# A two-layer decoder kernel: output products with high priority, expert results stored by block, residuals first in the last stage's memory

## The chip, the cores and the metric

The kernel runs on one core of a Trainium2 chip. The metric is the device time of one execution in microseconds; the lower the better. In the profile PE is the matrix engine, DVE the vector engine, ACT the scalar engine, POOL the GpSimd engine and SP the engine that issues most of the DMAs.

## The reference

Two layers on 2048 tokens of width 1024, batch 1. Each layer mixes tokens and then applies a mixture of experts, and both steps end in a layer norm of the scaled residual plus the result:

```python
x = layer_norm(alpha * x + mixer(x))       # layer 0: sliding-window attention, layer 1: latent attention
x = layer_norm(alpha * x + hier_moe(x))    # 32 experts in 4 groups, 2 per token, hidden width 512

xs = xt[tok_sorted]                        # tokens sorted by expert
hid = silu(ragged_dot(xs, w_gate, sizes)) * ragged_dot(xs, w_up, sizes)
ys = ragged_dot(hid, w_down, sizes) * weight[order]
out = segment_sum(ys, tok_sorted)          # back to the tokens, two rows each
```

All inputs and outputs are float32.

## The kernel before

**Numbers.** Matrix products take each float32 operand as a high and a low float16 half and make three products of them (`mm3`, L196 to L198; for the experts L898 to L900 and L914 to L916). ACT cuts off the high half (`wh`, L171) and DVE or POOL the low half (`wl`, L176 or L174).

**Stages.** Tokens come in 16 tiles of 128. For layer 0, `swa` (0 to some 470 us of the span) computes the attention and writes its transposed result `aoT` to the DRAM array `o`; `project` multiplies by the output weights, adds the residual, normalizes, routes, and scatters each token's row into the slots of its experts (array `xs`); `moe` (from some 706 us) runs 32 experts. For layer 1, `mla` first adds up the experts' results of layer 0, then attends (to some 2575 us), and `project` and `moe` (2820 to 3513 us) follow again. `combine_last` (from 3513 us) adds the two expert rows of each token to the residual, normalizes and writes the output.

**Slots.** Every expert has `SLOT` = 192 rows in `xs` and in its result array `y` (`y0` for layer 0, `y1` for layer 1). `CAPS` is the number of rows that the kernel computes for an expert: 184 for one, 176 for four, 160 for six, 152 for five, 144 for seven and 128 for nine, the larger ones for the experts with more tokens. Rows behind `CAPS` that hold tokens are treated by a loop (`overflow`) that runs only if there are any. In `swa` a DMA per expert (L401, two for each tile) clears the upper half of its `xs` rows.

**An expert.** Six weight pieces of 1 MB each (tile `raw`, five buffers, loaded by SP at L828) are cut into halves; `up` and `down` multiply; DVE transposes the result into `yr` (L918), and `store` writes it with four POOL DMAs (L926) of 192 KB, always all 6 blocks of 32 rows. `yr` is one of three fixed tiles, whose blocks behind the 128th row were cleared once per layer by POOL (L941).

**Output products.** In `project` (L263) the loads of tile t+2, the products of tile t and its norm are written in one loop (`skew`). `load` takes the attention's result `o` (two buffers) and the residual `pxr`; `gemm` makes two halves of 24 matmuls each and adds each half to `pxr` at L294. Only layer 0's first two loads of `o` are under `tc.high_priority()`.

**The last stage.** `combine_last` loads all 16 residual tiles `cz0` to `cz15` (L1090) ahead, gathers two rows for each token (`cy0`, `cy1`, nine buffers each; POOL, L1066), adds them (`cz`, two DVE operations at L1073), and normalizes. `layer_norm_shared` needs ACT twice, DVE at L248, L250 and L251, a reciprocal square root on POOL (`pow`, L252), and then DVE at L253.

**Order.** The order of the instructions on each engine is fixed when the kernel is built: the framework simulates a timeline with its own costs, and the instruction that is ready first in it, or has priority, goes first in the engine's queue. At run time each queue is strictly in order. A pool's place in memory decides which earlier tile's last use a new tile waits for, so pools matter for the order too.

Of the kernel before, what the change touches and what calls it, by code (L numbers as in the profile page):

```python
# [9 lines left out]
F32 = mybir.dt.float32  # L10
# [11 lines left out]
P = 128  # L22
# [98 lines left out]
class Kernel:  # L121
# [141 lines left out]
    def project(self, i, w_o, o_view, res, x_out, xs_d, rp, weights, early):  # L263

        nc, tc = self.nc, self.tc
        with ExitStack() as s:
# [10 lines left out]
            T, sent = {}, []  # L277

            def load(t):
                with tc.high_priority() if i == 0 and t < 2 else ExitStack():  # L280
                    ov = o_view(op, t)
                xr = self.t(wk, [P, D], F32, "pxr", bufs=3)
                nc.sync.dma_start(xr, res[t * P:(t + 1) * P, :])
                T[t] = {"o": ov, "xr": xr}

            def gemm(t):
                o, xr = T[t]["o"], T[t]["xr"]
                for n in range(2):
                    cs = slice(n * 512, (n + 1) * 512)
                    py = self.t(pm, [P, 512], F32, "mm")  # L290
                    for c in range(KC):
                        self.mm3(py, o[:, 0, c], o[:, 1, c], wh[c][:, cs], wl[c][:, cs], c == 0, c == KC - 1)

                    nc.vector.scalar_tensor_tensor(xr[:, cs], xr[:, cs], ALPHA * WS, py, op0=ALU.mult, op1=ALU.add)  # L294
# [63 lines left out]

        return (wh, wl), load

    def swa(self, xt_d, o_d, w_o, xs_d, keep):

        nc, tc, a = self.nc, self.tc, self.a
        V, G, C = nc.vector, nc.gpsimd, nc.scalar
# [1 line left out]
        with ExitStack() as s:  # L366
# [25 lines left out]

            zero = self.t(wk, [P, D], F16, "zero", bufs=1)
            G.memset(zero, 0.0)
            rooms, cleared = xs_d.rearrange("(e s) (u c) -> e s u c", s=SLOT, u=2)[:, SLOT // 2:], []

            def clear(t):
                one = T[t]["xl"][0:1, 0, 0:1]
                V.tensor_tensor(zero[0:1, 0:1], one, one, op=ALU.is_lt)
                for e in range(t, NE, NT):  # L400
                    cl = nc.sync.dma_start(rooms[e], zero[:SLOT // 2, None, :].to_broadcast([SLOT // 2, 2, D]))  # L401
                    for q in cleared:
                        tc.declare_no_dep(cl.ins, q.ins, reason="other rows")
                    cleared.append(cl)

            pick = self.after[:, None, :].bitcast(I32).to_broadcast([P, 2, P])
            upto = self.upto[:, None, :].to_broadcast([P, 8, P])
# [454 lines left out]
    def moe(self, i, x_d, xs_d, y_d, held, rp, weights, first):  # L862
# [3 lines left out]
        ids, blocks = rp["ids"], lambda e: -(-CAPS[e] // 32)  # L866
        xs = xs_d.rearrange("(e s) c -> e s c", s=SLOT)
        ys = y_d.rearrange("(e b i) (a k) -> e a i b k", b=CB, i=32, a=4)
        X, H = {}, {}
        with ExitStack() as s:  # L870
            wp = s.enter_context(tc.tile_pool(name=f"mw{i}", bufs=1, reuse_waits="tile"))
            xk = s.enter_context(tc.tile_pool(name=f"mx{i}", bufs=3, side="right", reuse_waits="tile"))
# [32 lines left out]

            def down(e, q):
                hh, hl = H[e]
                py, yr = pys[q], yrs[e % 3]
                for d in range(2):
                    out = py[:, d, :CAPS[e]]  # L910
                    cs = slice((2 * (q % 2) + d) * P, (2 * (q % 2) + d + 1) * P)
                    for m in range(F // P):
                        hi, lo = (w.rearrange("p (m d) -> p m d", m=F // P)[:, m, cs] for w in W[e, 4 + q // 2])
                        nc.tensor.matmul(out, hi, hh[:, m], start=m == 0, stop=False)  # L914
                        nc.tensor.matmul(out, hi, hl[:, m], start=False, stop=False)  # L915
                        nc.tensor.matmul(out, lo, hh[:, m], start=False, stop=m == F // P - 1)  # L916
                for d in range(2):
                    nc.vector.transpose(yr[:, :blocks(e), (2 * q + d) * 32:(2 * q + d + 1) * 32],  # L918
                                        py[:, d, :32 * blocks(e)].rearrange("p (b i) -> p b i", i=32))
                if q == 3:  # L920
                    store(e)

            def store(e):
                to = self.expert(ids, e, mybir.EngineType.Pool)
                for a in range(4):
                    st = nc.gpsimd.dma_start(ys[to, a].rearrange("o i b k -> (o i) b k"), yrs[e % 3][32 * a:32 * a + 32])  # L926
                    for q in stored:
                        tc.declare_no_dep(st.ins, q.ins, reason="other rows")
                    stored.append(st)
                for x in (H, X):  # L930
                    x.pop(e)

            stored = []
# [2 lines left out]
            pys = [self.t(ps, [P, 2, 256], F32, f"py{n}") for n in range(4)]  # L936
            for p in pys:
                nc.vector.memset(p[:, :, CAPS[0]:CAPB], 0.0)
            yrs = [self.t(wk, [P, CB, 256], F32, f"yr{n}", bufs=1) for n in range(3)]
            for y in yrs:  # L940
                nc.gpsimd.memset(y[:, min(CAPS) // 32:], 0.0)  # L941
            for u in range(4 * NE + BEHIND):
                e, m = divmod(u, 4)
                cut_to(u - 1)
# [135 lines left out]
    def combine_last(self, i, x_d, y_d, out):  # L1080
        nc, tc = self.nc, self.tc
        with ExitStack() as s:
            yp, c, zp, wk = (s.enter_context(tc.tile_pool(name=f"{n}{i}", bufs=bufs, reuse_waits="tile"))
                             for n, bufs in (("cy", 9), ("cl", 1), ("cz", 1), ("cw", 4)))
            T = [{} for _ in range(NT)]
            g, b = self.load_ln(c, i, 1)

            def load_x(t):
                T[t]["z"] = self.t(zp, [P, D], F32, f"cz{t}")
                nc.sync.dma_start(T[t]["z"], x_d[t * P:(t + 1) * P, :])  # L1090

            for t in range(NT):
                load_x(t)

            def load(t):
                self.combine_rows(t, yp, y_d, T[t])

            def norm(t):
                d = T[t]
                self.combine_sum(t, d)  # L1100
                if t > NT - 3:
                    self.layer_norm(wk, d["z"], d["x"], g, b, 1.0 / ALPHA)
                else:
                    self.layer_norm_shared(wk, d["z"], d["x"], g, b, 1.0 / ALPHA)
                nc.sync.dma_start(out[t * P:(t + 1) * P, :], d["x"])

            skew(NT, (load, 0), (norm, 6))
# [432 lines left out]

def scratch(k, pool):
    d = {n: k.t(pool, [rows, D], F32, n) for n, rows in
         (("x1", S), ("x2", S), ("x3", S), ("xc", S), ("y0", ROWS), ("y1", ROWS))}
    d["wd"] = k.t(pool, [2 * S, 1], F32, "wd")
    d["xs"] = k.t(pool, [ROWS, 2 * D], F16, "xs")
    d["o"] = k.t(pool, [NT, P, 2 * D], F16, "o")
    d["ob"] = k.t(pool, [KC, P, 2, S], F16, "ob")
    d["q"] = k.t(pool, [4, 3, P, 2, S], F16, "q")
    d["kr"] = k.t(pool, [ROPE, 2, S], F16, "kr")
    return d  # L1550
# [45 lines left out]
def trunk(tc, a, out):  # L1596
    with ExitStack() as ctx:
# [1 line left out]
        d = scratch(k, ctx.enter_context(tc.tile_pool(name="dram", bufs=1, space=DRAM)))  # L1599
        k.constants(ctx)  # L1600
        keep = ExitStack()
        w_o = k.swa(a["x_t"], d["o"], a["a_w_o"][0], d["xs"], keep)
        feed_forward(k, tc, 0, w_o, tile_of(k, d["o"]), a["x"][0], d["x1"], d["xs"], d["y0"], (d["xc"], d["wd"]), 7, keep)
        keep = ExitStack()
        w_o = k.mla(d["x1"], d["y0"], d["x2"], d, keep)
        feed_forward(k, tc, 1, w_o, chunk_of(k, d["ob"]), d["x2"], d["x3"], d["xs"], d["y1"], (d["xc"], d["wd"]), 5, keep)
        k.combine_last(1, d["x3"], d["y1"], out[0])


def expert_pieces(inputs):  # L1610
# [35 lines left out]
```

## Time and profile before

| | us |
|---|---|
| median of 3 runs | 3634.66 |
| lowest and highest | 3625.09, 3639.14 |
| the profiled execution | 3634.45 |
| its span, in which the rows' times count | 3632.5 |

The granted clock of PE is given as a share of full speed, 0.923 in the mean over the span. The rows below are of five kinds. In the page's slices each digit is a fortieth of the span, in tenths. In a table by stretch each engine has its busy microseconds and its number of instructions, and behind them stand the granted clock, the DMA engines' share and their rate. In lists of waits a row has the waiting engine and line, what ended the wait, the sum, the count and the longest. In a timeline a row has the start, the duration, engine, line, operation, tiles written and read, how many in a row, and in brackets the idle time before it with what ended that. An issue row of SP (SPq) tells when SP handed a DMA over, and not how long the transfer took.

### The profile page before, as it was taken

Reading aid. Unit: us, or ns where it says so; the run is one execution under the profiler, and the core shown is the slowest. Engines: PE = TensorE matmul, PEld = TensorE weight load, DVE = VectorE, ACT = ScalarE, POOL = GpSimd, SP = SyncE. Lnnn points to the kernel's source line nnn. Section 1 sums busy time; section 2 is a strip of 40 time slices with the busy share of each in tenths; the row PEclk is TensorE's granted clock in tenths of the full one; section 3 lists DMA queues with packets and bytes.
Section 4 is the critical chain, followed back from the end, with each engine's and each line's share of the span. In section 5 each row is a group of like instructions: output and inputs, shape, how many; then the busy total and the mean of one; then the engine's idle time right before and its main releaser. Section 6 shows DMA issues by size and latency. Waiting matters only on the chain. (4 is left out here: it accounts for less than half of the span.)

```text
span 3632.5 us, 83064 instructions
## 1 busy us (share of the span) xinstructions
PE 2978.4 (82%) x32611; PEld 2241.4 (62%) x32611; DVE 2765.4 (76%) x5272; ACT 2109.8 (58%) x3669; POOL 1563.2 (43%) x1568
## 2 busy tenths in 40 slices
PE   7888788699988885688898888888886899888850
PEld 3445443399988884344566556565443899888850
DVE  5777767788777786675788888788586788787758
ACT  6666621266666774443777777677210666666743
POOL 3545334322222335564576666566144133322344
PEclk9999899799998997899999999999998899999975
DMA  7877679899999998997899999899698999999995
GB/s 209 173 167 154 134 225 313 257 346 339 343 354 359 358 360 270 223 219 183 140 194 182 171 167 178 160 181 188 175 302 243 281 363 350 361 359 361 355 355 207
DMA packets 1108729, 931.59 MB, mean 256 GB/s; under 512 B 933120, under 2 KB 991744, under 8 KB 1057408
## 3 DMA queue, kind: packets, MB, share of 16 engines
q1 hardware_dynamic: 1073504, 808.65, 83.3%
q0 software_dynamic: 34816, 117.47, 8.9%
q8 instruction: 259, 4.24, 0.5%
q14 instruction: 150, 1.23, 0.1%
HBM read 538.32 MB, written 159.65 MB: 192 GB/s over the span
## 5 line engine op out<-in xcount | busy, mean ns | idle before, releaser
L176 DVE SCALAR_TENSOR_TENSOR wl<-raw,wh 128x2048 f16<-128x2048 f32 x322 | 838.7, 2608 | 196.5 <-ACT wh L171 196.3
L898 PE MATMUL pg<-xt,wh 128*128 128x128 f16 (+5 forms) x4096 | 827.7, 232 | 58.9 <-DMA xt<-xs 28.1
L900 PE MATMUL pg<-xt,wl 128*128 128x128 f16 (+5 forms) x4096 | 814.7, 232 | 46.4 <-DVE wl L176 46.3
L899 PE MATMUL pg<-xt,wh 128*128 128x128 f16 (+5 forms) x4096 | 827.4, 232 | 0.0
L171 ACT ACTIVATE wh<-raw 128x2048 f16<-128x2048 f32 x384 | 723.9, 1901 | 117.1 <-DMA raw<-in_moe_w_dram 112.6
L1416 POOL TENSOR_TENSOR bpp<-bpr,bpp 128x512 f16<-128x512 f32 (+3 forms) x448 | 474.2, 1077 | 273.8 <-DVE bpp L1413 173.3
L916 PE MATMUL py<-hh,wl 128*128 128x128 f16 (+5 forms) x2048 | 415.2, 231 | 48.7 <-POOL wl L174 48.7
L926 POOL DMA_DIRECT2D y<-yr x256 | 145.3, 569 | 716.0 <-DVE yr L918 424.0
L900 PEld LDWEIGHTS <-wl 128*128 128x128 f16 x4096 | 405.6, 100 | 57.9 <-DVE wl L176 57.7
L898 PEld LDWEIGHTS <-wh 128*128 128x128 f16 x4096 | 408.1, 100 | 44.9 <-issue 31.1
L1389 DVE TENSOR_REDUCE bsm<-sc 128x1 f32<-128x512 f32 (+3 forms) x640 | 373.1, 601 | 80.4 <-PE sc L1386 60.3
L899 PEld LDWEIGHTS <-wh 128*128 128x128 f16 x4096 | 408.4, 100 | 17.0 <-issue 17.0
L915 PE MATMUL py<-hl,wh 128*128 128x128 f16 (+5 forms) x2048 | 414.8, 230 | 4.6 <-DVE hl L174 4.5
L914 PE MATMUL py<-hh,wh 128*128 128x128 f16 (+5 forms) x2048 | 413.8, 230 | 1.6 <-ACT wh L171 1.3
L1398 ACT ACTIVATE bpr<-sc,bsm 128x512 f32<-128x512 f32 (+3 forms) x640 | 352.5, 630 | 90.4 <-DVE bsm L1394 84.4
L174 POOL TENSOR_TENSOR wl<-raw,wh 128x2048 f16<-128x2048 f32 x62 | 253.4, 4087 | 266.1 <-ACT wh L171 244.9
L1447 PE MATMUL po<-v,bpt 128*128 128x130 f16 x1750 | 205.3, 223 | 79.5 <-DMA bpt<-bpp 72.8
L1384 PE MATMUL sc<-kb,qb 96*128 96x512 f16 (+3 forms) x640 | 232.8, 364 | 29.8 <-DVE ro L1289 12.4
L916 PEld LDWEIGHTS <-wl 128*128 128x128 f16 x2048 | 202.9, 99 | 60.1 <-POOL wl L174 55.0
L1385 PE MATMUL sc<-kb,qb 96*128 96x512 f16 (+3 forms) x640 | 232.3, 363 | 0.0
L1386 PE MATMUL sc<-kb,qb 96*128 96x512 f16 (+3 forms) x640 | 230.8, 362 | 0.0
L1447 PEld LDWEIGHTS <-bpt 128*128 128x128 f16 x1750 | 160.0, 98 | 112.0 <-DMA bpt<-bpp 94.7
(324 smaller groups left out, 7771.7 us busy)
## 6 DMA issues: line engine op xcount, KB each, us to landing
raw<-in_moe_w_dram SPq DMA_DIRECT2D x384, 1024.0 KB
y<-yr POOLq DMA_DIRECT2D x256, 192.0 KB
x<-pxr SPq DMA_DIRECT2D x32, 512.0 KB
cz<-x SPq DMA_DIRECT2D x32, 512.0 KB
xs<-zero SPq DMA_DIRECT2D x32, 384.0 KB
q<-qn SPq DMA_DIRECT2D x48, 256.0 KB
ax<-in_x_t_dram SPq DMA_DIRECT2D x16, 512.0 KB
o<-aoT SPq DMA_DIRECT2D x16, 512.0 KB
```

The source lines that it names most:

```text
L171: nc.scalar.activation(hi, src, AF.Copy, scale=scale)
L176: eng.scalar_tensor_tensor(lo, src, scale, hi, op0=ALU.mult, op1=ALU.subtract)
L898: nc.tensor.matmul(out, hi, x[:, c], start=c == 0, stop=False)
L899: nc.tensor.matmul(out, hi, x[:, KC + c], start=False, stop=False)
L900: nc.tensor.matmul(out, lo, x[:, c], start=False, stop=c == KC - 1)
L914: nc.tensor.matmul(out, hi, hh[:, m], start=m == 0, stop=False)
L915: nc.tensor.matmul(out, hi, hl[:, m], start=False, stop=False)
L916: nc.tensor.matmul(out, lo, hh[:, m], start=False, stop=m == F // P - 1)
L1389: V.tensor_reduce(sm[:, c:c + 1], sc[:, :w], axis=AX.X, op=ALU.max, negate=ncn == 1)
L1398: C.activation(pr[:, :w], sc[:, :w], AF.Exp, bias=nm)
L1416: (V if mine[1] else G).tensor_tensor(pp[:, :, 1], pb, pp[:, :, 0], op=ALU.subtract)
L1447: nc.tensor.matmul(po, pt[:, k % 4, 0], vv, start=k == 0, stop=False)
```

## The change

In `project` the loads of `o` and of the residual and the products of tiles 0 and 1 get high priority in both layers. The results `y0` and `y1` become one array `y`; `store` writes only the blocks of 32 rows that `CAPS` of the expert covers, so that of 192 blocks per layer 36 (of 128 KB each) are no longer written, and `yr` becomes an ordinary tile of a pool with three buffers without clearing. Instead `swa` clears rows 128 to 191 of each expert in `y` (two DMAs of 256 KB per tile, 32 in all). In `combine_last` the pools are opened in another order, so that the residuals `cz` take the lowest addresses and `cy` the place they had.

```diff
@@ project @@
             def load(t):
-                with tc.high_priority() if i == 0 and t < 2 else ExitStack():
+                with tc.high_priority() if t < 2 else ExitStack():
                     ov = o_view(op, t)
-                xr = self.t(wk, [P, D], F32, "pxr", bufs=3)
-                nc.sync.dma_start(xr, res[t * P:(t + 1) * P, :])
+                    xr = self.t(wk, [P, D], F32, "pxr", bufs=3)
+                    nc.sync.dma_start(xr, res[t * P:(t + 1) * P, :])
                 T[t] = {"o": ov, "xr": xr}

             def gemm(t):
+                with tc.high_priority() if t < 2 else ExitStack():
+                    product(t)
+
+            def product(t):
                 o, xr = T[t]["o"], T[t]["xr"]
@@ swa @@
+            least, swept = min(CAPS) // 32 * 32, []
+            sums = y_d.rearrange("(e s) (u c) -> e s u c", s=SLOT, u=2)[:, least:]
...
+                    cl = nc.sync.dma_start(sums[e], zero.bitcast(F32).rearrange("p (u c) -> p u c", u=1)[:SLOT - least].to_broadcast([SLOT - least, 2, D // 2]))
+                    for q in swept:
+                        tc.declare_no_dep(cl.ins, q.ins, reason="other rows")
+                    swept.append(cl)
@@ moe @@
             def down(e, q):
                 hh, hl = H[e]
-                py, yr = pys[q], yrs[e % 3]
+                if q == 0:
+                    Y[e] = self.t(wk, [P, CB, 256], F32, "yr", bufs=3)
+                py, yr = pys[q], Y[e]
...
-                    st = nc.gpsimd.dma_start(ys[to, a].rearrange("o i b k -> (o i) b k"), yrs[e % 3][32 * a:32 * a + 32])
+                    st = nc.gpsimd.dma_start(ys[to, a, :, :blocks(e)].rearrange("o i b k -> (o i) b k"), Y[e][32 * a:32 * a + 32, :blocks(e)])
...
-            yrs = [self.t(wk, [P, CB, 256], F32, f"yr{n}", bufs=1) for n in range(3)]
-            for y in yrs:
-                nc.gpsimd.memset(y[:, min(CAPS) // 32:], 0.0)
@@ combine_last @@
-            yp, c, zp, wk = (s.enter_context(tc.tile_pool(name=f"{n}{i}", bufs=bufs, reuse_waits="tile"))
-                             for n, bufs in (("cy", 9), ("cl", 1), ("cz", 1), ("cw", 4)))
+            zp, c, yp, wk = (s.enter_context(tc.tile_pool(name=f"{n}{i}", bufs=bufs, reuse_waits="tile"))
+                             for n, bufs in (("cz", 1), ("cl", 1), ("cy", 9), ("cw", 4)))
@@ scratch @@
-         (("x1", S), ("x2", S), ("x3", S), ("xc", S), ("y0", ROWS), ("y1", ROWS))}
+         (("x1", S), ("x2", S), ("x3", S), ("xc", S), ("y", ROWS))}
```

The order that is built moves at these places. First SP's queue where layer 0's attention ends. `apt` and `aoT` are transposes by DMA of the last attention tiles, `o<-aoT` a store of the attention's result, `o_...<-o` the loads for the first products, `lng`, `lnb` and `wr` constants of the norm and the router. Line numbers of the changed kernel are higher: its L1574 is L1565, its L543 is L533. Before:

```order
L180 DMA_TRANSPOSE aoT_1007_5762<-aop_1006_5759 128x16x128
L1565 DMA o_1045_5927<-o_9_65 128x2048
L1565 DMA o_1047_5931<-o_9_65 128x2048
L180 DMA_TRANSPOSE apt_993_5657<-app_992_5654 128x8x128
L180 DMA_TRANSPOSE apt_1001_5710<-app_1000_5707 128x8x128
L533 DMA o_9_65<-aoT_1007_5762 128x2048
L219 DMA lng_1049_5935<-in_ln_g_dram 128x1024
L220 DMA lnb_1050_5936<-in_ln_b_dram 128x1024
L258 DMA wr32_1051_5939<-in_moe_w_group_dram 128x8x4
```

With the change:

```order
L1574 DMA o_1044_5958<-o_8_64 128x2048
L1574 DMA o_1046_5962<-o_8_64 128x2048
L219 DMA lng_1048_5966<-in_ln_g_dram 128x1024
L220 DMA lnb_1049_5967<-in_ln_b_dram 128x1024
L258 DMA wr32_1050_5970<-in_moe_w_group_dram 128x8x4
L180 DMA_TRANSPOSE apt_992_5688<-app_991_5685 128x8x128
L180 DMA_TRANSPOSE aoT_1006_5793<-aop_1005_5790 128x16x128
L180 DMA_TRANSPOSE apt_1000_5741<-app_999_5738 128x8x128
L543 DMA o_8_64<-aoT_1006_5793 128x2048
```

Three constants and one `aoT` now stand ahead of the last transposes of the attention. On PE the first output product stands in both kernels behind the last attention matmul, in both layers.

Second DVE's queue in the last stage, from its first sum to the first L253, which waits for POOL's first `pow`. L1082 of the changed kernel is L1073. Before, all of it:

```order
L1073 SCALAR_TENSOR_TENSOR cz0_6311_53116<-cy0_6327_53148,w12_23_95,cz0_6311_53116 128x1024
L1073 SCALAR_TENSOR_TENSOR cz0_6311_53116<-cy1_6328_53152,w12_23_95,cz0_6311_53116 128x1024
L248 TENSOR_SCALAR lnms_6341_53206<-lnms_6341_53206 128x1
L250 SCALAR_TENSOR_TENSOR cz0_6311_53116<-cz0_6311_53116,lnms_6341_53206,lng_6309_53112 128x1024
L251 TENSOR_SCALAR lnms_6341_53206<-lnms_6341_53206 128x1
L1073 SCALAR_TENSOR_TENSOR cz1_6312_53118<-cy0_6329_53156,w12_23_95,cz1_6312_53118 128x1024
L1073 SCALAR_TENSOR_TENSOR cz1_6312_53118<-cy1_6330_53160,w12_23_95,cz1_6312_53118 128x1024
L248 TENSOR_SCALAR lnms_6345_53226<-lnms_6345_53226 128x1
L253 SCALAR_TENSOR_TENSOR cz0_6311_53116<-cz0_6311_53116,lnms_6341_53206,lnb_6310_53113 128x1024
```

With the change, its last rows up to the first L253:

```order
L1082 SCALAR_TENSOR_TENSOR cz4_6372_53207<-cy1_6393_53267,w12_22_94,cz4_6372_53207 128x1024
L1082 SCALAR_TENSOR_TENSOR cz5_6373_53209<-cy0_6394_53271,w12_22_94,cz5_6373_53209 128x1024
L250 SCALAR_TENSOR_TENSOR cz3_6371_53205<-cz3_6371_53205,lnms_6410_53349,lng_6366_53195 128x1024
L251 TENSOR_SCALAR lnms_6410_53349<-lnms_6410_53349 128x1
L1082 SCALAR_TENSOR_TENSOR cz6_6374_53211<-cy0_6396_53279,w12_22_94,cz6_6374_53211 128x1024
L1082 SCALAR_TENSOR_TENSOR cz5_6373_53209<-cy1_6395_53275,w12_22_94,cz5_6373_53209 128x1024
L253 SCALAR_TENSOR_TENSOR cz0_6368_53199<-cz0_6368_53199,lnms_6398_53289,lnb_6367_53196 128x1024
```

Before, four sums and one L250 stand ahead of the first L253; now thirteen sums (tiles 0 to 5 and one of tile 6) and four L250. On POOL 20 gathers stand ahead of the first `pow` before, and 22 now.

## Rows read from the trace of the kernel before

**Rows 1.** Page, part 2: the span in 40 slices.
```profile
DMA  7877679899999998997899999899698999999995
```

**Rows 2.** Table by stretch (us; busy and count per engine; clock, DMA share, GB/s).
```profile
200.00:300.00 100.00, 86.48 (x596) 48.60 (x593) 75.52 (x181) 69.69 (x242) 46.83 (x73) 0.91 0.85 173
```

**Rows 3.** Timeline of SP in `swa`: clears of three tiles, and a weight load.
```profile
113.79 0.33 SPq L356 DMA_DIRECT2D worw<-in_a_w_o_dram  x1
114.21 1.27 SPq L401 DMA_DIRECT2D xs<-zero  x2
...
304.84 1.27 SPq L401 DMA_DIRECT2D xs<-zero  x2
...
387.09 1.28 SPq L401 DMA_DIRECT2D xs<-zero  x2
```

**Rows 4.** Waits from 50 to 440 us: waits for transposes by DMA.
```profile
DVE apt L504 <- DMA apt<-app: 66.1, 40, 3.6
...
PE sc L484 <- DMA qT<-qs: 27.1, 13, 3.7
```

**Rows 5.** Timelines of SP and of PE where layer 0's attention ends.
```profile
461.28 3.36 SPq L180 DMA_TRANSPOSE apt<-app  x2
...
465.47 0.44 SPq L219 DMA_DIRECT2D lng<-in_ln_g_dram  x1
...
465.81 0.29 PE L516 MATMUL po<-vv,apt 128*128 128x128 f16 x1 [5.76 <-DMA apt<-app]
```

**Rows 6.** Waits of DVE from 466 to 520 us: the first residual of layer 0.
```profile
DVE pxr L294 <- DMA pxr<-in_x_dram: 8.6, 1, 8.6
```

**Rows 7.** Timeline of PE, layer 1's first output products.
```profile
2578.84 0.61 PE L196 MATMUL mm<-ck,o 128*128 128x512 f16 x1 [6.53 <-DMA o<-ob]
...
2584.05 0.38 PE L196 MATMUL mm<-ck,o 128*128 128x512 f16 x1
2584.27 0.38 PE L197 MATMUL mm<-kst,o 128*128 128x512 f16 x1
```

**Rows 8.** Table by stretch, columns as in rows 2: the experts.
```profile
760.00:900.00 140.00, 139.43 (x2047) 139.29 (x2046) 116.41 (x135) 93.98 (x100) 44.90 (x35) 1.00 1.02 347
900.00:1100.00 200.00, 183.27 (x2691) 179.42 (x2688) 155.38 (x203) 132.86 (x140) 57.63 (x49) 0.97 1.05 348
1100.00:1300.00 200.00, 174.09 (x2629) 169.38 (x2630) 156.67 (x194) 137.09 (x139) 58.82 (x46) 0.94 1.03 355
2880.00:3215.00 335.00, 318.31 (x4661) 314.65 (x4659) 268.47 (x338) 227.57 (x236) 99.84 (x83) 0.98 1.05 358
```

**Rows 9.** Waits from 2880 to 3215 us: for weight pieces.
```profile
ACT wh L171 <- DMA raw<-in_moe_w_dram: 15.2, 18, 1.6
...
ACT raw L841 <- DMA raw<-in_moe_w_dram: 8.4, 8, 3.2
```

**Rows 10.** Timeline of POOL in the last stage.
```profile
3520.54 1.12 POOL L1066 DMA_INDIRECT cy<-y,iy  x1 [6.69 <-DMA y<-yr]
...
3527.59 1.97 POOL L1066 DMA_INDIRECT cy<-y,iy  x1 [0.30 <-issue]
3529.86 0.99 POOL L1066 DMA_INDIRECT cy<-y,iy  x1 [0.30 <-issue]
...
3547.78 0.59 POOL L252 TENSOR_TENSOR lnms<-lnms,half 128x1 f32<-128x1 f32 x1
```

**Rows 11.** Timeline of DVE in the last stage.
```profile
3527.41 1.28 DVE L1073 SCALAR_TENSOR_TENSOR cz<-cy,w,cz 128x1024 f32<-128x1024 f32 x1 [0.99 <-DMA cy<-y,iy]
...
3548.41 1.28 DVE L253 SCALAR_TENSOR_TENSOR cz<-cz,lnms,lnb 128x1024 f32<-128x1024 f32 x1 [11.80 <-POOL lnms L252]
3549.61 1.28 DVE L250 SCALAR_TENSOR_TENSOR cz<-cz,lnms,lng 128x1024 f32<-128x1024 f32 x1
```

**Rows 12.** Table by stretch, columns as in rows 2: the last stage from 3555 us.
```profile
3555.00:3590.00 35.00, 0.00 (x0) 0.00 (x0) 31.51 (x40) 16.75 (x29) 19.59 (x15) 0.50 0.68 235
3590.00:3632.00 42.00, 0.00 (x0) 0.00 (x0) 37.83 (x48) 11.72 (x20) 12.96 (x9) 0.50 0.31 125
```

More of the change, by code (lines that the diff above doesn't have):

```diff
@@ L359, in output_weights, with swa @@
         return (wh, wl), load
-    def swa(self, xt_d, o_d, w_o, xs_d, keep):
+    def swa(self, xt_d, o_d, w_o, xs_d, y_d, keep):
         nc, tc, a = self.nc, self.tc, self.a
@@ L868, in moe @@
         ys = y_d.rearrange("(e b i) (a k) -> e a i b k", b=CB, i=32, a=4)
-        X, H = {}, {}
+        X, H, Y = {}, {}, {}
         with ExitStack() as s:
@@ L929, in store @@
                     stored.append(st)
-                for x in (H, X):
+                for x in (H, X, Y):
                     x.pop(e)
@@ L1601, in trunk @@
         keep = ExitStack()
-        w_o = k.swa(a["x_t"], d["o"], a["a_w_o"][0], d["xs"], keep)
-        feed_forward(k, tc, 0, w_o, tile_of(k, d["o"]), a["x"][0], d["x1"], d["xs"], d["y0"], (d["xc"], d["wd"]), 7, keep)
+        w_o = k.swa(a["x_t"], d["o"], a["a_w_o"][0], d["xs"], d["y"], keep)
+        feed_forward(k, tc, 0, w_o, tile_of(k, d["o"]), a["x"][0], d["x1"], d["xs"], d["y"], (d["xc"], d["wd"]), 7, keep)
         keep = ExitStack()
-        w_o = k.mla(d["x1"], d["y0"], d["x2"], d, keep)
-        feed_forward(k, tc, 1, w_o, chunk_of(k, d["ob"]), d["x2"], d["x3"], d["xs"], d["y1"], (d["xc"], d["wd"]), 5, keep)
-        k.combine_last(1, d["x3"], d["y1"], out[0])
+        w_o = k.mla(d["x1"], d["y"], d["x2"], d, keep)
+        feed_forward(k, tc, 1, w_o, chunk_of(k, d["ob"]), d["x2"], d["x3"], d["xs"], d["y"], (d["xc"], d["wd"]), 5, keep)
+        k.combine_last(1, d["x3"], d["y"], out[0])
 def expert_pieces(inputs):
```

## The prediction

> **What bounds the kernel now.** I began with the page's slices [rows 1]: the DMA engines are near full in several stages, and the digits drop to half only at the very end. The change touches four stages, so I read each by itself, in the table by stretch and then in the waits.
>
> In `swa` PE is busy 86 of 100 us and DVE 76 while DMA has a share of 0.85 at only 173 GB/s [rows 2]: many small transfers. Waits on transposes by DMA are spread over the stage, 66.1 us on DVE and 27.1 on PE [rows 4]. A later transposition can therefore matter here.
>
> In the experts two things are full at once [rows 8]. DMA has a share of 1.02 to 1.05 at 347 to 358 GB/s, and PE is busy 139.4 of 140, 183.3 of 200, 174.1 of 200 and 318.3 of 335 us. ACT, which makes a weight piece's high half, waits for pieces to land, 15.2 and 8.4 us in the fourth stretch [rows 9].
>
> In the last stage PE is done. POOL's first gather starts at 3520.54, 6.69 us after its last store was issued [rows 10]. DVE stands still for 11.80 us, until POOL has made its first `pow` at 3547.78 [rows 10, 11]. From 3555 us DVE is busy 31.51 of 35 and 37.83 of 42 us [rows 12]: it is the bound there, and what it could have done while it stood still would come off the end.
>
> **Part by part.** *Last stage.* The new pool order changes what the framework's timeline believes about the residuals' loads, and so DVE's queue. Before, 4 sums and one L250 (five large operations) stand ahead of the first L253; now 13 sums and four L250, which is 17. Such an operation takes 1.28 us and the next starts 1.20 us later [rows 11]. So 12 x 1.20 = 14.4 us of work move into the standstill. Against this, POOL has 22 gathers instead of 20 ahead of its first `pow`. The 20 took 3547.78 - 3520.54 = 27.24 us, 1.36 each, so two more cost 2.7. And a gather is slower beside a sum: the one at 3527.59 took 1.97 us, the one after it, with DVE waiting, 0.99 [rows 10, 11]. Twelve more operations at up to 0.98 would be 11.8 us. But five operations in that stretch had cost little: 20 gathers at 0.99 + 0.30 would be 25.8 us, and they took 27.24, 0.3 for each operation. Twelve at 0.3 are 3.6. The sum is -14.4 + 2.7 + 3.6 = -8.1. The short waits of DVE after 3548 (31.51 of 35 busy) should shrink as more sums lie between, which I put at 2 of those 3.5 us: **-10**. The ends are -14.4 + 2.7 - 3.5 = -15 and -14.4 + 2.7 + 11.8 = 0.
>
> *Stores.* Each layer writes 36 x 128 KB = 4.7 MB less, at 355 GB/s 13.3 us of transfer [rows 8]. That is the upper end, 26.6 us for both layers. The lower end is nothing: from 760 to 900 us PE lost 0.6 us while DMA was just as full. A loss is excluded, since the same DMAs are only shorter. In the fourth stretch PE is idle for 16.7 us and ACT's waits for pieces sum to 23.6 [rows 8, 9], so the two are linked at most in part. I take a quarter of the transfer time, 3 us a layer: **-6**. The last four stores, which the first gather waits for, lose 256 KB together, 0.7 us at most, and are in this. The clearing of `yr` that falls away lies on POOL ahead of experts, where POOL is busy a third of the time [rows 8]: 0. One array `y` for both layers adds waits on gathers of layer 0, over for hundreds of us by then: 0.
>
> *Clears.* 32 DMAs of 256 KB join `swa`: 8.4 MB, at the 350 GB/s of rows that are full [rows 8] 24 us, and 32 issues of 0.64 us (two take 1.27 [rows 3]), 20 us of SP. All on the path that would be 44 us. The nearest experiment is in the trace itself. Every tile has two clears of 384 KB; tiles up to 304.84 us also have two weight loads of 256 KB, and later tiles have none. From 114.21 to 304.84 are seven tiles, 27.2 us each; from 304.84 to 387.09 three, 27.4 us each [rows 3]. So 512 KB per tile more, as much as the change adds, cost nothing that shows. I take **+3**, with 0 and 44 as the ends; nothing in it can gain.
>
> *First products.* The order shows that they do not move ahead of the attention's end: PE begins them behind its last attention matmul in both layers. What moves is around them. In layer 0 three constants' loads (two of 512 KB) and a transposition now stand ahead of the last `apt` transposes on SP. PE was waiting 5.76 us for just these [rows 5]. Two 512 KB loads at 350 GB/s are 3 us, three issues of 0.44 are 1.3, and a transposition as long as the issue of two [rows 5] would be 3.4: at most 7.7. The low end is 0, since the loads could be out of the way in the wait before. I take **+4**. The halves of tiles 0 and 1 alternate now, so by the order tile 0 is complete some 47 matmuls later in layer 0; DVE waited 8.6 us for the residual there anyway [rows 6], and the residual comes no earlier in the queue: 0. In layer 1 it is complete 18 matmuls later, at 0.22 us each [rows 7] 4 us; DVE has work of tile 1 meanwhile: **+2**, between 0 and 4.
>
> **Sum.** -10 - 6 + 3 + 4 + 2 = -7, on the profiled execution's 3634.45 us: **3627.5 us**. The median of the runs is 0.2 us higher, which changes nothing. About 0.5%, 18 us, is what a measurement of this kernel can tell from no change, so this counts as no change. The forecast's own range is 3616 to 3638.
>
> **Rivals.** *A, the clears sit in the path: slower.* SP's queue is strict. Each tile's transposes are issued behind the tile's clears, and PE and DVE wait for transposes [rows 4]. If each tile's two new clears push them back by their full transfer time, 512 KB at 350 GB/s is 1.5 us, by 16 tiles 24 us; with two issues of 0.64 us each tile it is 44. Instead of +3: 3648 to 3668, say 3657. It decides from 28 us on the path upward, where the time passes 3652.6. For it: the chain runs through these waits, and DMA is busy for 0.85 of the time [rows 2]. Against it: the even tiles of rows 3. The Trainium skill (DMA: Bandwidth & Descriptors, Queues, rings and completion order) says that an engine takes one queue's descriptors in ring order, which is this case; by it alone the forecast would be 3648. Rows 3 speak against it being the whole story, as the weight loads are on the same queue. Chance 0.15.
>
> *B, the experts are bound by DMA: faster.* With a share above 1 the DMA engines have no slack [rows 8], and if each saved byte counts, it is -26.6 rather than -6: 3607. Against it is the first stretch, with DMA full and PE never waiting. Chance 0.18.
>
> *C, the last stage gives nothing back.* Each operation of DVE beside a gather slows it as the 1.97 us one was, POOL's first `pow` comes 14.5 us later, and the standstill moves instead of shrinking: +10 on the forecast, 3637.5. The Trainium skill (GPSIMD Engine Reference, Specifications) has POOL share its memory interfaces with VectorE, with contention when a VectorE instruction has two inputs in SBUF, as each sum has. The trace agrees for the gather at 3527.59 (1.97 us) and not for most others. Chance 0.20.
>
> *D, nothing of the priority works* is no rival of its own: the order shows it, and the sum has it.
>
> **How the numbers follow.** The forecast's case has 0.47, of it 0.05 below 3616.4. Faster by over 0.5% is B (nearly all its 0.18) and that: 0.23. Slower by over 0.5% (above 3652.6) is most of A and some of the upper end of the first products on top: 0.13. Same is the rest, 0.64. For 8 in 10 the range must take in half of B, whose centre is 3607, and A's first half, up to 3650; what is left out is 0.08 below and 0.09 above.
>
> **What would show it.** The last stage: DVE's longest wait is 3 to 8 us, not 11.8, with 13 sums ahead; from the first gather to the end of the span it is some 102 us, where it was 112 (3632.5 - 3520.54). Experts: ACT's waits for pieces shorten by several us, the two stages by 2 to 4 us each. `swa`: the period from clear to clear stays within 0.5 us of 27.2; if it grows by 1.5 or more, A is right. Layer 0's seam: PE's wait for `apt` grows from 5.8 to some 10 us. The prediction is wrong if a stage not named here moves by over 5 us, or if the seam in layer 1 changes the attention's end.

## The result and the profile after

Beside four runs of the kernel before (median 3629.88 us) four runs of the changed kernel had a median of 3591.78 us (3582.10 to 3594.12): 0.9891 of before, 95% interval 0.9856 to 0.9926. Two later comparisons gave 0.9897 (0.9856 to 0.9938) and 0.9884 (0.9865 to 0.9903). So it is 38 to 47 us faster, some 1.1%, where I had forecast 7 us and a range from 3616 to 3638 us. The sign was right and the size far off.

Both kernels were traced again (two traces of before, three of the changed kernel). I cut each trace at the same events: the last attention product and the first expert product of each layer, the last expert product, and the first score of layer 1. Lengths in us:

| stage | before | changed | difference of means | predicted |
|---|---|---|---|---|
| attention of layer 0 | 468.9, 474.1 | 479.9, 479.7, 478.2 | +7.8 | +3, and +4 at its seam |
| project, layer 0 | 242.2, 246.8 | 239.1, 237.2, 237.5 | -6.6 | 0 |
| experts, layer 0 | 679.9, 677.8 | 672.9, 668.7, 669.0 | -8.6 | -3 |
| latents | 328.6, 316.8 | 309.7, 308.4, 313.8 | -12.1 | 0 |
| latent attention | 850.7, 849.6 | 861.1, 858.1, 853.8 | +7.5 | 0 |
| project, layer 1 | 262.1, 267.9 | 247.8, 247.8, 247.5 | -17.3 | +2 |
| experts, layer 1 | 677.9, 678.2 | 668.4, 669.5, 668.6 | -9.2 | -3 |
| last stage | 122.2, 121.5 | 113.3, 112.3, 113.7 | -8.8 | -10 |

The latents of before's first trace, 328.6 us, are an outlier: seven kernels further down that leave this stage's work as it is took 305 to 315, where the changed kernel is. So the -12.1 of this row is not the change's. The other rows repeat within some 7 us.

The page's slices after, as in [rows 1]:

```profile
DMA  8988779899999998996799999999699899999996
```

The first five slices, the attention of layer 0, are each a tenth fuller. The same stretches by the table, columns as in [rows 2] (the expert stretches are shifted with their stage):

```profile
200.00:300.00 100.00, 80.47 (x588) 46.40 (x588) 73.02 (x176) 65.90 (x229) 46.55 (x73) 0.94 0.91 192
765.00:905.00 140.00, 137.63 (x2005) 137.37 (x2003) 113.79 (x137) 90.31 (x97) 41.20 (x35) 1.00 1.05 347
905.00:1105.00 200.00, 185.35 (x2747) 182.09 (x2745) 155.66 (x202) 136.26 (x143) 61.52 (x50) 0.98 1.05 345
1105.00:1305.00 200.00, 175.46 (x2734) 169.91 (x2732) 162.44 (x199) 139.91 (x143) 59.09 (x46) 0.97 1.05 356
2860.00:3195.00 335.00, 318.29 (x4698) 315.06 (x4696) 268.02 (x337) 226.57 (x235) 102.00 (x82) 0.99 1.04 357
```

Against [rows 8] PE's busy time is nearly the same, and so is DMA's rate, 345 to 357 GB/s. What rose, but for the first of them (2005 for 2047), is the number of matmuls in the same time: 2747 for 2691, 2734 for 2629, 4698 for 4661. The rate stayed and each expert needs fewer bytes. ACT's waits for weight pieces from 2860 to 3195 us, which were 15.2 and 8.4 us [rows 9], are shorter, as I had said they would be:

```profile
ACT wh L171 <- DMA raw<-in_moe_w_dram: 9.3, 11, 1.5
ACT raw L851 <- DMA raw<-in_moe_w_dram: 1.7, 2, 1.3
```

These waits do not go with the stage's length, though. In the same 335 us of the stage, one kernel further down that stores all blocks (the priority's second trace) has 10.8 and 4.0 us and a stage of 679.6 us, and one that stores by block (stores and clears without the rest) has 20.9 and 6.2 us and a stage of 665.4.

The clears in the attention of layer 0, as in [rows 3]; seven tiles lie between the first two rows, and three between the last two:

```profile
113.52 0.63 SPq L407 DMA_DIRECT2D xs<-zero  x1
...
311.92 0.63 SPq L407 DMA_DIRECT2D xs<-zero  x1
...
396.23 0.62 SPq L407 DMA_DIRECT2D xs<-zero  x1
```

A tile takes 28.3 and then 28.1 us, where it took 27.2 and 27.4. In before's second trace it took 27.8 up to the second of these clears, in the other two traces of the changed kernel 28.3 and 28.5. PE's last waits for `apt` at the seam of layer 0, as in [rows 5]:

```profile
474.26 0.29 PE L526 MATMUL po<-vv,apt 128*128 128x128 f16 x1 [5.41 <-DMA apt<-app]
...
478.14 0.29 PE L526 MATMUL po<-vv,apt 128*128 128x128 f16 x1 [1.85 <-DMA apt<-app]
```

The last stage: POOL's first gather, one beside DVE's large operations (an L250 began at 3512.95 us, sums follow it), the 22nd, the first `pow`, and then DVE's longest waits, as in [rows 10, 11]:

```profile
3489.16 1.12 POOL L1075 DMA_INDIRECT cy<-y,iy  x1 [6.70 <-DMA y<-yr]
...
3513.00 2.09 POOL L1075 DMA_INDIRECT cy<-y,iy  x1 [0.30 <-issue]
...
3521.89 0.99 POOL L1075 DMA_INDIRECT cy<-y,iy  x1 [0.30 <-issue]
3522.91 0.60 POOL L252 TENSOR_TENSOR lnms<-lnms,half 128x1 f32<-128x1 f32 x1
```

```profile
3523.54 1.28 DVE L253 SCALAR_TENSOR_TENSOR cz<-cz,lnms,lnb 128x1024 f32<-128x1024 f32 x1 [6.86 <-POOL lnms L252]
...
3530.04 1.28 DVE L253 SCALAR_TENSOR_TENSOR cz<-cz,lnms,lnb 128x1024 f32<-128x1024 f32 x1 [1.64 <-POOL lnms L252]
```

DVE's long stop is 6.86 us and was 11.80. The `pow` starts 33.75 us after the first gather (3522.91 - 3489.16), before 27.24. From the first L253 to the end of the span it is 68.6 us, before 84.1.

### The profile page after: what moved, and what is told of

Read it like the earlier page. It is cut to its first block, busy times and chain, and to the rows that moved or that the text cites. A ratio compares the mean times of both kernels' runs of the same rounds, so it can differ in the third digit from the quotient of the medians.

```text
span 3592.2 us, 83083 instructions
## 1 busy us (share of the span) xinstructions
PE 2973.6 (83%) x32611; PEld 2239.1 (62%) x32611; DVE 2767.1 (77%) x5272; ACT 2109.6 (59%) x3669; POOL 1576.8 (44%) x1562
```

## Experiments

**Before, once more.** The same program.

> The kernel before once more, for a second trace of it. If single stages of one kernel differ by over 5 us from trace to trace, the stage differences seen between the two kernels (attention of layer 0 +12.8 us, latents about -19, latent attention +10, project of layer 1 about -14) can be chance; if they agree within 3 us, they belong to the change.

One run took 3634.73 us; the stages are in the table above. The stages of the two traces differ by up to 6 us, the latents by 12. So a single stage's difference under 6 us in a single trace says nothing, and latents need several.

**The priority alone, twice.**

```diff
-                with tc.high_priority() if i == 0 and t < 2 else ExitStack():
+                with tc.high_priority() if t < 2 else ExitStack():
...
             def gemm(t):
+                with tc.high_priority() if t < 2 else ExitStack():
+                    product(t)
```

> Only the edits in project. Theory: the priority, by moving the loads of o and of the residual on SP's queue, makes the 14 us that project of layer 1 lost: the whole is 12 to 20 us faster, project of layer 1 14 us shorter, and the layer-0 seam some 0 to 5 us longer. Rival (my prediction's reading): first products cost 2 to 6 us and gain nothing, the project of layer 1 got shorter from something else: 0 to 6 us slower.

3623.24 us against 3628.78: 0.9979 (0.9954 to 1.0005). Project took 239.5 us in layer 0, but 263.8 in layer 1: neither theory's pattern. At tile 9 of layer 1 this trace was even with the changed kernel (140.7 and 140.4 us behind the last attention product). Then one transposition held SP for 15.34 us, in the changed kernel 8.85, and the seven loads of `o` behind it for 12.79 us instead of 7.11:

```profile
2697.09 15.34 SPq L180 DMA_TRANSPOSE pxt<-pxp  x1
2712.48 12.79 SPq L1583 DMA_DIRECT2D o<-ob  x7
```

```profile
2703.06 8.85 SPq L180 DMA_TRANSPOSE pxt<-pxp  x1
2711.97 7.11 SPq L1588 DMA_DIRECT2D o<-ob  x7
```

The first two rows are the priority's, the others the changed kernel's. Together they are 12 of the 16 us between the two stages. What held SP longer was not found. As SP, DVE and PE have the same order there in both, the same program was run again:

> The priority alone once more, beside the one above on the same chip: if its 264 us in the project of layer 1 were chance, this trace shows some 248; if not, 258 to 266.

3604.73 us against 3631.51: 0.9932 (0.9907 to 0.9958), and project of layer 1 took 249.5 us. So the 263.8 were not the program's; over all twelve traces with this priority or with its products' part that stage takes 246 to 264 us, and 262 to 269 in the six without. In layer 0 it takes 237 to 242 us in eleven with it (the one with clears in that stage left out) and 242 to 249 in the six without. PE's waits in project, of layer 0 in the second trace of this kernel (470 to 709 us) and of layer 1 (2558 to 2802 us):

```profile
PE pre L632 <- DVE occ L630: 21.4, 7, 5.0
...
PE pl L196 <- DMA pxt<-pxp: 2.9, 2, 1.5
...
PE pre L632 <- DVE occ L630: 10.2, 4, 5.1
...
PE pl L196 <- DMA pxt<-pxp: 6.0, 5, 3.9
```

Before, PE waited for the router's transposed rows (`pxt`) and for the routing's counts of tokens per expert (`occ`, from DVE) in layer 0 (470 to 710 us) and in layer 1 (2575 to 2832 us):

```profile
PE pl L196 <- DMA pxt<-pxp: 17.1, 5, 10.9
PE pre L628 <- DVE occ L626: 12.7, 3, 5.2
...
PE pl L196 <- DMA pxt<-pxp: 19.8, 7, 7.9
PE pre L628 <- DVE occ L626: 14.8, 5, 5.0
```

In layer 0 the waits for `pxt` fell by 14.2 us and those for `occ` rose by 8.7, which leaves 5.5 us; the stage is 5.5 shorter than the mean of before's two traces. By the two ratios the priority is worth 8 us, with an interval that takes in no change, and 25 us. The stages that are shorter are the two of project.

**One array only.** The priority and the two result arrays made one, against the run just told, on the same chip.

```diff
-         (("x1", S), ("x2", S), ("x3", S), ("xc", S), ("y0", ROWS), ("y1", ROWS))}
+         (("x1", S), ("x2", S), ("x3", S), ("xc", S), ("y", ROWS))}
...
```

> The priority alone, as before, with the two result arrays made one (all six blocks stored, no clears); every engine's order is that of the priority alone, only addresses in DRAM differ. Theory: with one array the project of layer 1 takes 246 to 251 us as in the changed kernel, where the priority alone took 264, and the kernel is 10 us or more faster than the priority alone. Rival: one array does nothing; project of layer 1 stays at 258 to 266, and the two are within 4 us.

3608.77 us (0.9934, 0.9914 to 0.9953); project of layer 1 took 255.3 us, between what theory and rival said. By the time the two are 4 us apart, and this one is the slower: no gain from addresses shows.

**The products' priority alone.**

```diff
             def gemm(t):
+                with tc.high_priority() if t < 2 else ExitStack():
+                    product(t)
...
```

> The kernel before with high priority for the products of tiles 0 and 1 alone, none for further loads. Theory: the alternated halves put the first router products behind three tiles of output products instead of two, so PE waits less for the transposed rows of the router; then the project of layer 0 is 239 us long (before 242 to 247) and PE's waits for them there fall from 17 us to below 6, as with all of the priority. Rival: it is the loads of o that come earlier on SP's queue: then it stays at 242 to 247.

One run, 3612.88 us. Project of layer 0 took 238.7 us, as with all of the priority, PE waited 0.4 us for `pxt` in it, and project of layer 1 took 258.0. So for layer 0 the products' priority is enough, with none for further loads; for layer 1 one trace does not tell. But it also moves loads: SP's queue has the loads for tiles 2 and 3 together, ahead of the first transposition of `pxt`, where before the one for tile 3 stood behind it. Before:

```profile
482.39 0.38 SPq L1565 DMA_DIRECT2D o<-o  x1
...
493.51 1.94 SPq L180 DMA_TRANSPOSE pxt<-pxp  x1
495.50 0.99 SPq L1565 DMA_DIRECT2D o<-o  x1
```

With the priority (its first trace; with the products' alone the order is the same):

```profile
493.30 0.80 SPq L1569 DMA_DIRECT2D o<-o  x2
499.76 1.52 SPq L304 DMA_DIRECT2D x<-pxr  x2
...
503.06 4.13 SPq L180 DMA_TRANSPOSE pxt<-pxp  x1
```

**The router one tile later**, without the change. This moves the router's products on PE and leaves the order of the first loads on SP as before; the router's input `pxt` gets three buffers, the scatter's `pxp` five.

```diff
-            skew(NT, (load, 0), (start, 1), (gemm, 2), (norm, 2), (experts, 2), (router, 3), (route, 3))
+            skew(NT, (load, 0), (start, 1), (gemm, 2), (norm, 2), (experts, 2), (router, 4), (route, 4))
```

> The kernel before with nothing of the change; instead the router stage of the project loop comes one tile later (and one more buffer for its input, one less for its scatter's). Theory: more output products ahead of a router product on PE are all that the priority gave; project of layer 0 is 4 to 8 us shorter, that of layer 1 6 us or more. Rival: the wait for the transposed rows is not what sets the pace, and both stay within 3 us.

0.9995 (0.9972 to 1.0019); project took 244.1 and 268.6 us, in the fastest of ten executions. PE's wait for `pxt` in layer 0 did fall, from 17.1 to 9.8 us, and nothing came of it: in its place PE waited 7.0 us on DVE. In layer 1 (2549 to 2812 us) it fell from 19.8 us to none, and the wait for `occ` doubled from 14.8:

```profile
PE pre L628 <- DVE occ L626: 29.8, 7, 8.8
```

So taking the waits for `pxt` away is not enough. But a later router also makes `occ` later, so this does not show that they are no cause. SP's order of loads, the products' order on PE, or both are left; they were not parted.

**The router later on top of the change**, the same line in the changed kernel.

> The changed kernel with the router stage one tile later, as above. If both act on the same wait, it is within 4 us of the changed kernel; if the later router works for all tiles where the priority works for the first ones, 5 to 12 us faster.

3606.96 us, 0.9936 (0.9910 to 0.9962), where the changed kernel has 0.9884 to 0.9897: some 15 us slower, which neither expectation has. The traced execution was the fastest of seven (3595.81 us); its stages are within 4 us of the changed kernel's but for the latents (320.4), so it cannot show where the 15 us lie. Not followed further.

**Clears, stores by block and one array, without the rest.**

```diff
+                    cl = nc.sync.dma_start(sums[e], zero.bitcast(F32).rearrange("p (u c) -> p u c", u=1)[:SLOT - least].to_broadcast([SLOT - least, 2, D // 2]))
...
-                    st = nc.gpsimd.dma_start(ys[to, a].rearrange("o i b k -> (o i) b k"), yrs[e % 3][32 * a:32 * a + 32])
+                    st = nc.gpsimd.dma_start(ys[to, a, :, :blocks(e)].rearrange("o i b k -> (o i) b k"), Y[e][32 * a:32 * a + 32, :blocks(e)])
```

> Only the clears in the attention of layer 0, the stores by block and the one result array. Theory: the clears cost 10 to 13 us in the attention of layer 0, each expert stage gains 7 to 9 us, and the latents move by 15 us or more because their order changes: 10 to 20 us faster in all. Rival: the latents' gain is not from this part: then clears and stores cancel, within 6 us of no change.

3622.43 us, 0.9978 (0.9955 to 1.0001): 8 us faster, between theory and rival, with an interval that takes in no change. The attention of layer 0 took 481.5 us, the experts 668.5 and 665.4 (10 and 13 less, somewhat more than the theory's 7 to 9), the latents 312.5, as other kernels that leave them alone. The first two parts of the theory hold, the latents' does not. Project took 249.0 and 266.5 us, as before, so its gain is not from here.

**The clears alone.** All six blocks stored as before.

```diff
+                    cl = nc.sync.dma_start(sums[e], zero.bitcast(F32).rearrange("p (u c) -> p u c", u=1)[:SLOT - least].to_broadcast([SLOT - least, 2, D // 2]))
...
```

> The kernel before with the 32 new clears alone (of layer 0's result array; all six blocks are stored as before). Theory: the attention of layer 0 gets 8 to 12 us longer, by the clears alone, and both expert stages stay at 678 us within 4. Rival: the expert stages' 10 us were the order that changes with the clears, and the second expert stage, whose order changes here too, gets 8 us or more shorter without one byte less.

One run, 3620.40 us. Attention of layer 0 477.7 us, experts 675.6 and 684.9: the clears cost some 6 us, and the second expert stage with its other order is longer and not shorter. The order that the clears bring is not what made the experts faster.

**Half of the blocks**, with the clears from row 96 on. This kernel leaves out the results of slots behind the 96th.

```diff
-                    st = nc.gpsimd.dma_start(ys[to, a, :, :blocks(e)].rearrange("o i b k -> (o i) b k"), Y[e][32 * a:32 * a + 32, :blocks(e)])
+                    st = nc.gpsimd.dma_start(ys[to, a, :, :3].rearrange("o i b k -> (o i) b k"), Y[e][32 * a:32 * a + 32, :3])
```

> The changed kernel storing only 3 of 6 blocks of every expert (96 blocks fewer per layer than before instead of 36; results of slots behind the 96th are left out, and the clears take rows 96 to 191). Theory that the expert stages are bound by DMA bytes: 12.6 MB less than before at 355 GB/s is 35 us, so each expert stage is 20 us or more below before's 678, as far as PE lets it. Rival (the stage is PE's, DVE's and ACT's, and only little hangs on DMA): within 5 us of the changed kernel's 670. The attention of layer 0 is 3 to 6 us longer than the changed kernel's, by half as many bytes again.

One run, 3591.77 us. Experts 658.0 and 668.7 us, attention of layer 0 484.4. In layer 0 the bytes' theory holds: 12.6 MB less gave 21 us against before's mean of 679, 4.7 MB some 9. Against the changed kernel only the bytes of the stores and the larger clears differ. In layer 1 the further bytes gave nothing: there the stage stood at 669 already. What stops it there was not found; ACT's waits for pieces did not fall further but rose, from the changed kernel's 12.2 us to 27.8 (2860 to 3400 us in both). Project of layer 1 took 259.2 us here.

**No clears; layer 0 stores all blocks, layer 1 by block.** Layer 0 also has its three fixed `yr` tiles and their clearing by POOL again.

```diff
-                    st = nc.gpsimd.dma_start(ys[to, a, :, :blocks(e)].rearrange("o i b k -> (o i) b k"), Y[e][32 * a:32 * a + 32, :blocks(e)])
+                    n = CB if i == 0 else blocks(e)
+                    st = nc.gpsimd.dma_start(ys[to, a, :, :n].rearrange("o i b k -> (o i) b k"), Y[e][32 * a:32 * a + 32, :n])
```

> The changed kernel without clears: layer 0 stores all six blocks as before, and layer 1 alone stores by block into the one array. Theory (clears cost 8 us in the attention of layer 0, storing less gains 9 in the first expert stage): attention 471 us, first expert stage 678, the rest as in the changed kernel, the time within 5 us of it. Rival: if the first expert stage's gain was its order and not the bytes, it stays near 670 and this is 8 us faster than the changed kernel.

3590.15 us, 0.9891 (0.9863 to 0.9918), and the changed kernel beside it 3588.85: the same time. Attention of layer 0 471.5, experts 685.6 and 672.3. Each layer's experts follow their own stores. The other traces agree, the one with half of the blocks aside: where a layer stores all blocks its expert stage takes 674 to 686 us, where it stores by block 665 to 673, in either layer. That it is the bytes, and not the `yr` tiles that change with them, is shown for layer 0 by the run with half of the blocks, in one trace; for layer 1 it is not shown. The granted clock does not part them, 0.96 to 0.98 in the expert stages of both kinds, save one at 0.99. What goes with the stores is PE's waits for low halves (`wl`), in layer 0 here (760 to 1300 us) and then in the changed kernel (765 to 1305 us), before 17.6 and 18.7:

```profile
PE pg L906 <- DVE wl L176: 18.5, 23, 2.0
PE py L924 <- POOL wl L174: 16.7, 12, 1.9
```

```profile
PE pg L910 <- DVE wl L176: 15.9, 23, 2.0
PE py L928 <- POOL wl L174: 13.8, 10, 1.9
```

ACT's waits for pieces in the same stretches do not: 31.3 us before, 32.2 in both of these.

**The clears at the end of project**, behind the last tile's norm, from a zeroed tile of `pxp`, and none in the attention.

```diff
-            skew(NT, (load, 0), (start, 1), (gemm, 2), (norm, 2), (experts, 2), (router, 3), (route, 3))
+            skew(NT, (load, 0), (start, 1), (gemm, 2), (norm, 2), (experts, 2), (router, 3), (clear, 3), (route, 3))
...
```

> The changed kernel with the 32 clears moved from the attention of layer 0 to the end of its project stage, where SP waits 13 us for the routing and the DMA engines are half idle. Theory: the attention is 7 to 10 us shorter, the project stage up to 7 us longer: 2 to 8 us faster than the changed kernel in all. Rival: the clears were not what made the attention longer, or they push the experts' first rows back by their whole 24 us: no gain or slower.

3618.44 us, 0.9967 (0.9944 to 0.9990), some 27 us slower than the changed kernel. The attention was 471.0 us, so the 8 us were the clears; but project took 269.8 instead of 237 to 239. SP's timeline there:

```profile
680.69 51.14 SPq L350 DMA_DIRECT2D y<-pxp  x32
733.99 3.13 SPq L180 DMA_TRANSPOSE xt<-xs  x1
```

The 32 clears held SP for 51.14 us, 1.60 each, and the experts' first rows are loaded only behind them. That is 8.4 MB handed over at 164 GB/s, half the rate that I had counted with. In the attention the same 32 lengthened the stage by 8 us, a sixth of these 51; there SP stood some 32 us at them in all, and other work ran meanwhile.

**The pool order alone.**

```diff
-                             for n, bufs in (("cy", 9), ("cl", 1), ("cz", 1), ("cw", 4)))
+                             for n, bufs in (("cz", 1), ("cl", 1), ("cy", 9), ("cw", 4)))
```

> Only the pool order in the last stage; nothing before that stage is built otherwise. Theory: DVE's long standstill shrinks from 11.8 us to some 4, and the last stage is 8 to 10 us shorter. Rival: the gathers slow beside the sums as one of them did, and the stage is within 3 us of before.

0.9992 (0.9968 to 1.0015) by time, not told apart from nothing; by the trace the last stage took 114.9 us instead of 121.5 and 122.2. DVE's stop before its first L253 was 1.65 us. By the stage the theory holds at 7 us, a little short of its 8 to 10, and the rival does not.

**The change without the pool order**, and the changed kernel on the same chip.

> The change without the pool order of the last stage; everything before that stage is built as in the changed kernel. Theory: the pool order is worth 8 us wherever it stands, so this is 8 us slower than the changed kernel and the last stage 121 us long instead of 113; the rest of the stages as in the changed kernel within 5 us. Rival: the parts help each other, and without the pool order more than 15 us are lost.

> The changed kernel once more. If its gain belongs to it, the time is 30 to 42 us below before's, and project of layer 1 is again some 248 us long (last attention product to first expert product), 10 to 17 below before's 262 and 268. If those were chance in one trace, it is 258 to 266 and the whole gain nearer 20 to 25 us.

3604.14 us (0.9927, 0.9902 to 0.9952) and 3586.84 (0.9897). The last stage took 121.0 and 112.3 us, all stages before it agree within 5 us but the latents (321.1 and 308.4). So by the stage the pool order is worth 9 us here as well. The times are 17 us apart, which is the rival's over 15; but the two intervals overlap, and in the traces the rest lies in the latents, which the pool order does not touch. The third comparison of the changed kernel:

> The changed kernel on the same chip as the three above, for their comparison: 3582 to 3594 us, project of layer 1 248 us.

3588.85 us, 0.9884; project of layer 1 took 247.5 us.

**Whether a version beats it.** None did: the one without clears is as fast; the ones with the later router and with the clears at the end of project are slower.

## Why the prediction was wrong

The sum was -10 - 6 + 3 + 4 + 2 = -7. By the table the last stage gave -9, the experts -18, the attention of layer 0 +8 and the project stages -24. The greatest miss is the last of these: the sum had +2 for project, and +4 for the seam ahead of it.

- *Last stage, right.* I had 14.4 us moved into the stop, 2.7 for two more gathers and 3.6 for gathers slowed by sums. POOL's way to its first `pow` grew by 33.75 - 27.24 = 6.5 us, against 6.3 predicted, and the stage is 9 shorter, against 10: what follows the first L253 is 15.5 us shorter, nearly all of it the 14.4 us moved; DVE's short waits in it sum to 3.8 us instead of 4.0, so the 2 us that I had put there did not come. Four of 22 gathers took 2.0 to 2.1 us (one in the rows above), where one of 20 had; others beside sums still took 0.99. Slower gathers take back a quarter of the 14.4 us and not all of them: rival C was wrong. The Trainium skill (GPSIMD Engine Reference, Specifications) names contention on the shared interfaces for two inputs in SBUF; the four slow gathers agree with it, and the others do not.
- *Stores, mis-sized.* The step that failed is "I take a quarter of the transfer time, 3 us a layer". Measured are some 9 a layer of the 13.3 (10.5 and 11 by the means of all traces), nearer to rival B. I let one stretch weigh most, from 760 to 900 us, in which PE lost nothing while DMA was full. The other three rows of the same group, with PE idle for 5 to 13% under the same DMA rate, spoke the other way. The sign that I had named, ACT's waits for pieces, does not go with the gain; PE's waits for low halves do. Storing all blocks in layer 0 again gave its stage back, 685.6. The Trainium skill (DMA: Bandwidth & Descriptors, Specifications) gives about 358 GB/s as one core's limit to HBM; the expert rows stand at 345 to 358 in both kernels, which agrees, and by it I should have read them as being at the limit.
- *Clears, mis-sized.* +3 predicted, 8 measured; forecast and rival A lay on either side. The step that failed is that "512 KB per tile more [...] cost nothing that shows", taken over from the weight loads of [rows 3] to clears. The period from clear to clear, which was to stay within 0.5 us of 27.2, grew by about 1 us, less than the 1.5 of rival A, and so tile by tile and not at one place. A clear held SP for 1.60 us where 32 stood in a row; why it costs more beside other work than a load of the same bytes was not found. Of rival A's 24 to 44 us a third came true at most. By the rule of the Trainium skill (DMA: Bandwidth & Descriptors, Queues, rings and completion order) alone I had put 24 us; the stage's 8 do not bear that out.
- *First products, wrong in sign.* The seam that I charged with 4 us cost little: PE's wait for `apt` was 5.41 us and another of 1.85, before 5.76 [rows 5], and the attention with priority and no clears took 471 us. That the products do not move ahead of the attention's end was right. The step that failed is "What moves is around them", which I priced only for the last `apt` transposes and for tile 0's lateness; the rest of the project stages I put at nothing without a reason. I did not follow SP's queue past the first loads: the loads of `o` for the next tiles move ahead of the transposes. Both project stages gained, by 7 and by 17 us in the table. That it is the priority is shown by the runs that have it alone; by which of its moves, on PE or on SP, stays open.
- *The sum of the parts.* Priority (8 and 25 us in two comparisons), stores with clears (8, with an interval that takes in no change) and pool order (3 by time, 7 to 9 by the stage) come to 19 to 42, the whole to 38 to 47. That the parts help each other is not shown; their intervals are too wide for it. That the first forecast had the right sign is partly luck, as its project term had the wrong one.

Left open: the latent attention is some 9 us longer in the mean where layer 0 stores by block (854 to 861 us in eight traces, 841 to 856 in the ten where it stores all), and I know of no part that acts there.

## What to carry to other kernels

Where DMA has a share of 1 at a steady rate through a stage and the engines behind it idle in some stretches, do not let the one stretch without idling price the saved bytes: here the first 4.7 MB gave two thirds to four fifths of their transfer time, the next 7.9 MB half of theirs in one layer and nothing in the other. When products are moved, read the whole queue of the engine that issues loads, past the first tile, for what now stands ahead of a transfer that waits. A stage's length in one trace can be off by 12 us here: repeat the trace before explaining it.

## What the runs showed of the hardware

Clears that read 64 rows of 2 KB of zeros twice and write 64 rows of 4 KB in DRAM held SP for 1.60 us each when 32 stood in a row: 164 GB/s. In the expert rows shown, weight loads of 1 MB beside stores ran at 345 to 358 GB/s. An indirect DMA of POOL took 0.99 us at its shortest, and four of 22 beside DVE's 128x1024 operations 2.0 to 2.1. The same transposition in the same order held SP for 15.34 us in one trace and 8.85 in another, and the seven loads behind it for 12.79 and 7.11; the stage of the first trace was 16 us longer.
